# Row factors spread by two two-part products, first weights loaded in pieces by two queues, and an opening group's POOL products behind a quad's sums

## The chip, the cores and the metric

The kernel runs on one core of one Trainium2 chip. The metric is the device time of one execution in microseconds, the median of three runs. Times inside the kernel come from the trace of one profiled execution; there 0 is the start of its span. TensorE is called PE in the profile, VectorE DVE, ScalarE ACT, GpSimd POOL, and SP is the engine that issues most DMAs.

## The reference

One layer of a decoder trunk: 16 meta tokens and 2048 tokens of width 1024 are normalised and projected to eight groups of 512 columns; four of them feed a gated convolution, four a retention with rotary positions; the two results are joined, projected once more, added to the residual stream and normalised.

```python
hn = rms_norm(h, norm_g)
proj = jnp.einsum('bld,de->ble', hn, w_in)
cx, cb, cc, cg, q, k, v, rg = jnp.split(proj, N_PROJ, axis=-1)
conv_out = short_conv_branch(cx, cb, cc, conv_w) * jax.nn.silu(cg)
...
ret = head_group_norm(retention_chunkwise(qf, kf, vf), ret_norm_g)
ret_out = ret.astype(h.dtype) * jax.nn.silu(rg)
mixed = jnp.concatenate([conv_out, ret_out], axis=-1)
return h + jnp.einsum('ble,ed->bld', mixed, w_out)
```

`rms_norm` scales each token by the inverse root of its mean square (the *row factor* below) and each of the 1024 columns by a gain.

## The kernel before, in words

**Products.** All large products are made of fp32 numbers split into a high and a low part of type fp32r (`split`, `parts`): the high part is a rounded copy made by ScalarE, the low part the rest, made by VectorE. A product of 128x128 by 128x512 then takes three matmuls: low by high, high by low, high by high. Most products run as `quad`s: a 2x2 block product with seven instead of eight block products, whose sums of weights POOL makes (`stationary`; `summed[0]` is the last of a quad's four). The first two products of the first half of the tokens, and one at each later stage, run as `quad_plain`: eight block products without sums, in two passes over the tokens, each into two banks of PSUM: 2 passes x 2 banks x 8 tiles of 128 rows x 3 matmuls, 96 for one call. Four PSUM banks (`ps_proj`) serve these products, so the second `quad_plain` can begin only when the results of the first have been copied out of their banks (line 512 on ScalarE, line 507 on VectorE).

**The opening** (lines 909 to 945). `moving` loads the 16 blocks of x for the first half of the tokens and splits them, scaled by the column gain (line 113 ScalarE, line 114 VectorE; line 188 multiplies four blocks by the gain on ScalarE). `begin` loads the first group's weights and splits them (`plain_part`, lines 110 and 122). Ahead of them nine warming matmuls on a zeroed tile stand on TensorE (`warm_up`), behind ScalarE's first activation, which writes into the same tile (line 882). `normalise_meta` makes the meta tokens' factors (lines 405 to 420), `meta_products` multiplies weights by them (line 429). `block_sums` makes the sums of x blocks (line 185 on VectorE, and a subtraction of POOL's, line 122, tile `t`).

**Row factors** (`row_factors`, `spread_factors`, `spread`). The rows of x are loaded once more, two tiles of 128x512 for each 128 tokens (line 347), squared and summed on ScalarE (line 380), 16 times for 1024 tokens. From the sums of 512 tokens VectorE and POOL make one factor for each token (the power by POOL, line 305). To have the factors along the free dimension of every partition, `spread` multiplies the identity by the column of factors (line 312, VectorE), and one fp32 matmul with a column of ones (line 319) spreads the four diagonals of 128x128 over all partitions; ScalarE copies the result out and squares it (lines 322 and 324). It is called once for the meta tokens (16 columns) and four times for 512 tokens, twice in each half.

**The order of the work** is not written out: a scheduler orders each engine's queue by its own picture of the time, by the order of the program's text, and by `tc.issue_after`, which holds an instruction behind a named one. An engine works off its queue in that order.

**The opening group** (`group_plain`) is computed with the two plain products; what remains of it (`complete`, `close`) is done within the next unit: among it two products by the row factors on POOL (line 507, tile `c` by `rr`).

Of the kernel before, what the change touches and what calls it, by code (L numbers as in the profile page):

```python
# [28 lines left out]
RING, RAW, GEN, COPIES = 3, 8, 16, 4  # L29
WARM = 9  # L30
HIGH = 400
# [48 lines left out]
def hybrid_trunk(ctx: ExitStack, tc: tile.TileContext, t, out: bass.AP, chunk_decay):  # L80
# [23 lines left out]
    def brief(name="b"):  # L104
        return sb.tile([P, HB + 128], F32, name=name, tag="b", bufs=BRIEF)[:, :HB]

    def split(hi, lo, src, scale=None, eng=nc.vector):

        if scale is None:
            nc.scalar.copy(out=hi, in_=src)  # L110
            sub(eng, lo, src, hi.bitcast(F32))
            return
        nc.scalar.mul(hi, src, scale)
# [164 lines left out]
    def quad_plain(w, m, take, middle=None):  # L278

        for j in range(2):  # L280
            banks = [ps_proj() for _ in range(2)]
            for half in range(2):
                for kt in range(KH):
                    ks = slice(kt * P, (kt + 1) * P)
                    mh, ml = m[BLOCK[half][j]][kt]
                    for i in range(2):
                        wh, wl = w[2 * i + half]
                        for n, (a, b) in enumerate(((wl, mh), (wh, ml), (wh, mh))):
                            nc.tensor.matmul(  # L289
# [18 lines left out]
    def spread(col, n, dst, squares=None):  # L308

        a = col.shape[1]  # L310
        diag = sb.tile([P, HB], F32, name="rot", tag="rot", bufs=1).rearrange("p (a c) -> p a c", a=CH)
        nc.vector.tensor_tensor(
            out=diag[:n, :a, :n],
            in0=ident[:n, :n].rearrange("p (a c) -> p a c", a=1).broadcast_to([n, a, n]),
            in1=col.rearrange("p (a c) -> p a c", c=1).broadcast_to([n, a, n]),
            op=ALU.mult,
        )
        rp = ps_misc()
        nc.tensor.matmul(
            rp[:, : a * n].rearrange("p (a c) -> p a c", a=a), ones[:n].broadcast_to([n, P]), diag[:n, :a, :n], start=True, stop=True  # L320
        )
        nc.scalar.copy(out=dst, in_=rp[:, : a * n])
# [4 lines left out]
    ident = const.tile([P, P], F32, name="ident")  # L327
    ones = const.tile([P, 1], F32, name="ones")
    neg_half = const.tile([P, CH], F32, name="neg_half")
    meta_s = const.tile([P, KT, NMETA], F32, name="meta_s")  # L330
# [168 lines left out]
    def group_plain(g, m, f, meta, first, between, ahead):  # L499
# [30 lines left out]
        def complete():  # L530
# [4 lines left out]
            for j in range(2):  # L535
# [3 lines left out]
                nc.scalar.activation(gate, gate, AF.Silu)  # L539
                mul(nc.gpsimd, cs[j], cs[j], rr[j])  # L540

        def close():
            with tc.issue_after(turned[0].ins):
                for j in range(2):
# [270 lines left out]
    def output(pair, m, final_g):  # L815
# [41 lines left out]
        for i in range(2):  # L857
# [7 lines left out]
            for j in range(2):  # L865
# [9 lines left out]
                (nc.scalar if i == j and cuts[i] > 1 else nc.sync).dma_start(out[row : row + P, cs], y)  # L875

    make_identity(nc, ident)
    nc.gpsimd.memset(ones, 1.0)
    nc.gpsimd.memset(neg_half, -0.5)
    warm = const.tile([P, P], BF16, name="warm")  # L880
    nc.vector.memset(warm, 0.0)
    nc.scalar.activation(warm[:, 0:1], warm[:, 0:1], AF.Silu)

# [15 lines left out]

    warm_up(WARM)  # L900
    nc.sync.dma_start(gain, t["norm1_g"])
    factors = [[] for _ in range(NR)]
    held = {}
    for r in range(NR):
# [7 lines left out]
        if r == 0:  # L912
# [115 lines left out]
```

## Time and profile before

| what | value |
|---|---|
| median of 3 runs | 878.27 us (878.2 to 878.86) |
| the profiled execution | 878.86 us, its span 877.1 us |
| PE busy | 865.1 us, 99% of the span |
| DVE, ACT, POOL busy | 725.6, 472.3, 403.2 us |
| granted TensorE clock, mean | 0.998 |
| first matmul of a product | 6.29 us |
| first matmul of the first quad | 57.44 us |

A timeline row is start, length, engine, line, operation, output <- inputs, shapes and count; in brackets stands how long the engine was idle ahead of it and what ended that. A row of groups ends in the busy time, the mean length in ns, and the idle time ahead. A row of waits is the waiting engine with its tile and line, the one waited for, the sum, the count and the longest. A row of stretches has the stretch, its length, the busy time (and count) of PE, PEld, DVE, ACT and POOL, the granted clock, the DMA engines' share and GB/s. The opening and its row factors fill the first 57 of 877 us.

### The profile page before, as it was taken

To read this page: it belongs to the slowest core of one execution; us is meant where nothing else is said; L and a number is where in the kernel's file an instruction comes from. 1 tells how busy PE (TensorE), PEld (TensorE's weight loads), DVE (VectorE), ACT (ScalarE), POOL (GpSimd) and SP (SyncE) were. 2 spreads that over 40 slices of the span, in tenths; PEclk is the share of its full clock that TensorE was granted. 3 is DMA by queue.
4 is the path that set the end of the run, shared out by engine and by line. 5 is a ranking of instruction groups with operands and counts; after the bars stand their busy time and mean duration, and the time that the engine had idled before them with its cause. 6 is when DMAs were issued, how large, how long until landed. Compare 5 with 4: busy or idle time off the path is not lost.

```text
span 877.1 us, 12737 instructions
## 1 busy us (share of the span) xinstructions
PE 865.1 (99%) x4279; PEld 711.6 (81%) x4279; DVE 725.6 (83%) x1178; ACT 472.3 (54%) x873; POOL 403.2 (46%) x291
## 2 busy tenths in 40 slices
PE   8999999999999999999999999999999999999996
PEld 5777787878888778788888888888888888788885
DVE  6899888989887867999889898988767699757764
ACT  8665537364654645836464645544334475545453
POOL 0564242333235555552223323355646455877763
PEclk9999999999999999999999999999999999999999
DMA  9723224352556533935144353646222593555432
GB/s 331 230 72 83 64 71 136 113 151 96 124 189 180 184 117 111 307 109 146 52 112 149 97 166 84 207 108 206 72 72 61 164 352 115 175 165 184 155 121 84
DMA packets 110033, 125.31 MB, mean 143 GB/s; under 512 B 41424, under 2 KB 58128, under 8 KB 109968
## 3 DMA queue, kind: packets, MB, share of 16 engines
q1 hardware_dynamic: 109824, 124.24, 46.2%
q8 instruction: 34, 0.56, 0.3%
q14 instruction: 31, 0.25, 0.1%
q10 hardware_dynamic: 144, 0.26, 0.1%
HBM read 90.92 MB, written 25.17 MB: 132 GB/s over the span
## 4 chain that ended last, share of the span: by engine, by line
PE 87%; DVE 4%; DMA 3%; issue 2%; ACT 1%; SPq 1%; POOL 1%; POOLq 0%; DVEq 0%; ACTq 0%
PE pj L232 71%; PE pj L289 7%; PE ms L773 2%; PE ms L774 2%; PE ms L763 2%; PE ms L750 2%; DVE ml L122 1%; DMA x<-in_xT 1%; DMA w<-in_w_out 1%; PE ms L429 1%; PE ms L741 1%; SPq L393 1%; DVE ml L114 1%; DVE wl L122 1%; DMA ra<-mixed 1%
## 5 line engine op out<-in xcount | busy, mean ns | idle before, releaser
L232 PE MATMUL pj<-mh,wl 128*128 128x512 f32 x1008 | 398.6, 395 | 1.3 <-DVE wl L122 1.2
L232 PE MATMUL pj<-mh,wh 128*128 128x512 f32 x1008 | 393.2, 390 | 0.0
L232 PE MATMUL pj<-ml,wh 128*128 128x512 f32 x1008 | 392.7, 390 | 0.0
L110 ACT CAST wh<-ra 128x512 fp32r<-128x512 f32 x216 | 133.8, 620 | 266.8 <-PE pj L232 216.2
L232 PEld LDWEIGHTS pj<-mh,wl 128*128 128x128 f32 x1008 | 189.3, 188 | 44.0 <-issue 2.6
L122 DVE TENSOR_TENSOR wl<-ra,wh 128x512 fp32r<-128x512 f32 x216 | 192.2, 891 | 39.3 <-ACT wh L110 38.3
L232 PEld LDWEIGHTS pj<-mh,wh 128*128 128x128 f32 x1008 | 189.2, 188 | 39.9
L232 PEld LDWEIGHTS pj<-ml,wh 128*128 128x128 f32 x1008 | 189.4, 188 | 38.1 <-issue 0.5
L119 POOL TENSOR_TENSOR sa<-ra 128x512 f32<-128x512 f32 x36 | 54.9, 1525 | 102.1 <-DVE wl L122 42.2
L122 POOL TENSOR_TENSOR ra<-sa,ra 128x512 f32<-128x512 f32 x36 | 54.6, 1517 | 76.9 <-DVE wl L122 73.0
L122 POOL TENSOR_TENSOR ra<-ra 128x512 f32<-128x512 f32 x36 | 56.2, 1562 | 60.5 <-PE ms L429 51.6
L149 POOL TENSOR_TENSOR ra<-ra 128x512 f32<-128x512 f32 x36 | 57.3, 1593 | 32.4 <-issue 22.8
L239 ACT COPY tc<-pj 128x512 f32<-128x512 f32 x108 | 62.5, 579 | 0.0
L289 PE MATMUL pj<-ml,mh 128*128 128x512 f32 x128 | 50.3, 393 | 0.1
L289 PE MATMUL pj<-mh,mh 128*128 128x512 f32 x128 | 50.1, 392 | 0.0
L289 PE MATMUL pj<-mh,ml 128*128 128x512 f32 x128 | 49.0, 399 | 1.0 <-DVE ml L122 0.5
L786 POOL TENSOR_TENSOR rp<-rs,neg_half 128x4 f32<-128x4 f32 x16 | 17.8, 1111 | 56.0 <-DVE rs L119 55.9
L565 POOL TENSOR_TENSOR c<-c,rr 128x512 f32<-128x512 f32 x14 | 29.4, 2101 | 25.6 <-DVE c L606 14.4
L842 DVE TENSOR_TENSOR yo<-pj,yo 128x512 f32<-128x512 f32 (+1 forms) x33 | 22.0, 670 | 18.4 <-POOL yo L119 10.9
L844 ACT ACTIVATE rot<-yo 128x512 f32<-128x512 f32 (+1 forms) x33 | 20.3, 616 | 30.7 <-DVE yo L842 30.2
L565 POOL TENSOR_TENSOR c<-c,tc 128x512 f32<-128x512 f32 x14 | 27.8, 1988 | 18.0 <-ACT tc L591 14.9
L848 POOL TENSOR_TENSOR z<-yo,final_g 128x512 f32<-128x512 f32 x16 | 26.8, 1678 | 16.5 <-DVE yo L842 16.5
(140 smaller groups left out, 1215.4 us busy)
## 6 DMA issues: line engine op xcount, KB each, us to landing
ra<-in_w_in SPq DMA_DIRECT2D x128, 256.0 KB, 2.8
x<-in_xT SPq DMA_DIRECT2D x48, 256.0 KB, 4.7
w<-in_w_out SPq DMA_DIRECT2D x32, 256.0 KB, 5.1
ra<-mixed SPq DMA_DIRECT2D x32, 256.0 KB, 2.9
yo<-in_x SPq DMA_DIRECT2D x32, 256.0 KB, 4.5
ra<-in_x SPq DMA_DIRECT2D x16, 256.0 KB, 3.2
mixed<-c SPq DMA_DIRECT2D x16, 256.0 KB, 2.6
mixed<-qg SPq DMA_DIRECT2D x16, 256.0 KB, 2.3
```

The costliest lines, as they stand in the source:

```text
L110: nc.scalar.copy(out=hi, in_=src)
L119: eng.tensor_tensor(out=out, in0=a, in1=b, op=ALU.add)
L122: eng.tensor_tensor(out=out, in0=a, in1=b, op=ALU.subtract)
L149: summed[0] = nc.gpsimd.tensor_tensor(out=a12, in0=a12, in1=a11, op=ALU.subtract)
L232: nc.tensor.matmul(bank, a[:, ks], b, start=first and kt == 0 and n == 0, stop=kt == KH - 1 and n == 2, skip_group_check=not first,)
L239: copied[0] = nc.scalar.copy(out=c, in_=bank)
L289: nc.tensor.matmul(banks[i], a[:, ks], b, start=half + kt + n == 0, stop=half == 1 and kt == KH - 1 and n == 2,)
L565: eng.tensor_tensor(out=out, in0=a, in1=b, op=ALU.mult)
L786: nc.gpsimd.tensor_tensor(out=rp, in0=rs, in1=neg_half.rearrange("p (c a) -> p c a", a=1), op=ALU.pow)
L842: last[0] = nc.vector.tensor_tensor(out=y[:, cs], in0=pp[:, cs], in1=y[:, cs], op=ALU.add)
L844: nc.scalar.activation(junk[:, cs], y[:, cs], AF.Square, accum_out=at)
L848: nc.gpsimd.tensor_tensor(out=ys[i][j], in0=y, in1=final_g[:, j * HB : (j + 1) * HB], op=ALU.mult)
```

## The change

**Spread.** The factors are split in a high and a low part first (two instructions on 128x4, VectorE); the low part's diagonals are made by VectorE in one instruction as before, the high part's by ScalarE in one instruction for each 128 tokens, into a tile of their own; two fp32r matmuls with a column of ones in fp32r add them up. **Opening.** The column gains and the first 128 columns of two of the first weight tiles are loaded by ScalarE's queue, ahead of its activation table; the other 384 columns by SP, and the splits of these tiles are cut the same way. Warming takes ten matmuls and no longer waits for ScalarE. In `quad_plain` high by high comes first. `normalise_meta` is called after the twelfth x block instead of the eighth; the sums of x blocks are held behind the eighth scaled copy. **POOL.** The opening group's two products by the row factors move from `complete` to `close`, behind `summed[0]`.

```diff
-WARM = 9
+WARM = 10
...
-        nc.scalar.mul(hi, src, scale)
+        scaled.append(nc.scalar.mul(hi, src, scale))
...
-                        for n, (a, b) in enumerate(((wl, mh), (wh, ml), (wh, mh))):
+                        for n, (a, b) in enumerate(((wh, mh), (wl, mh), (wh, ml))):
...
     def spread(col, n, dst, squares=None):
 
         a = col.shape[1]
-        diag = sb.tile([P, HB], F32, name="rot", tag="rot", bufs=1).rearrange("p (a c) -> p a c", a=CH)
+        high, low = (small.tile([P, CH], t, name="ch", tag=f"ch{t}")[:n, :a] for t in (F32R, F32))
+        nc.vector.tensor_copy(out=high, in_=col)
+        sub(nc.vector, low, col, high.bitcast(F32))
+        diags = [sb.tile([P, HB], F32R, name="rot", tag="rot", bufs=1), gen("dg")[:, :HB].bitcast(F32R)]
+        lows, highs = (d.rearrange("p (a c) -> p a c", a=CH)[:n, :a, :n] for d in diags)
         nc.vector.tensor_tensor(
-            out=diag[:n, :a, :n],
+            out=lows,
...
-            in1=col.rearrange("p (a c) -> p a c", c=1).broadcast_to([n, a, n]),
+            in1=low.rearrange("p (a c) -> p a c", c=1).broadcast_to([n, a, n]),
             op=ALU.mult,
         )
+        for c in range(a):
+            nc.scalar.mul(highs[:, c], ident[:n, :n], high[:, c : c + 1].bitcast(F32))
         rp = ps_misc()
-        nc.tensor.matmul(
-            rp[:, : a * n].rearrange("p (a c) -> p a c", a=a), ones[:n].broadcast_to([n, P]), diag[:n, :a, :n], start=True, stop=True
-        )
+        for d, first in ((highs, True), (lows, False)):
+            nc.tensor.matmul(
+                rp[:, : a * n].rearrange("p (a c) -> p a c", a=a), ones_r[:n].broadcast_to([n, P]), d,
+                start=first, stop=not first,
+            )
...
-                mul(nc.gpsimd, cs[j], cs[j], rr[j])
 
         def close():
+            with tc.issue_after(summed[0].ins):
+                for j in range(2):
+                    mul(nc.gpsimd, cs[j], cs[j], rr[j])
...
+    nc.scalar.dma_start(gain, t["norm1_g"])
+
+    PIECES = slice(0, P), slice(P, HB)
+    opening = {n: raw() for n in (0, 2)}
+    for n, a in opening.items():
+        nc.scalar.dma_start(a[:, PIECES[0]], t["w_in"][2 * NG, n][:, PIECES[0]])
...
-    nc.scalar.activation(warm[:, 0:1], warm[:, 0:1], AF.Silu)
+    function = const.tile([P, 1], BF16, name="function")
+    nc.scalar.activation(function, warm[:, 0:1], AF.Silu)
...
-    nc.sync.dma_start(gain, t["norm1_g"])
...
             def begin(half):
-                for n in (half, 2 + half):
-                    w[n] = plain_part(n, loads[n], FIRST_W)
+                if half:
+                    for n in (1, 3):
+                        w[n] = plain_part(n, loads[n], FIRST_W)
+                    return
+                for n, a in opening.items():
+                    w[n] = a, operand(FIRST_W, n)
+                    nc.sync.dma_start(a[:, PIECES[1]], t["w_in"][2 * NG, n][:, PIECES[1]])
+                done = []
+                for cs in PIECES:
+                    with ExitStack() as behind:
+                        for ins in done:
+                            behind.enter_context(tc.issue_after(ins.ins))
+                        for n, a in opening.items():
+                            hi, lo = w[n][1]
+                            done = [
+                                nc.scalar.copy(out=hi[:, cs], in_=a[:, cs]),
+                                nc.vector.tensor_tensor(
+                                    out=lo[:, cs], in0=a[:, cs], in1=hi[:, cs].bitcast(F32), op=ALU.subtract
+                                ),
+                            ]
...
-                load_x(r), gain_of, {(0, 0): lambda: begin(0), (0, KH - 1): lambda: begin(1), (0, KT - 1): normalise_meta}
+                load_x(r), gain_of, {(0, 0): lambda: begin(0), (0, KH - 1): lambda: begin(1), (1, KH - 1): normalise_meta}
...
-                block_sums(b11, b12, b22, b21, t1[kt], t3[kt], gain_of(kt), gain_of(KH + kt), nc.gpsimd)
+                with tc.issue_after(scaled[KT - 1].ins):
+                    block_sums(b11, b12, b22, b21, t1[kt], t3[kt], gain_of(kt), gain_of(KH + kt), nc.gpsimd)
```

With its inputs changed, the scheduler orders the opening anew. On TensorE, at the second spread of 512 tokens in before (line 319, from the tile `rot`); line 289 are the plain products, tiles `mh` and `ml` the high and low parts, line 429 the meta products:

```order
L289 MATMUL pj<-mh_240,mh_292 128x512
L289 MATMUL pj<-mh_240,ml_299 128x512
L289 MATMUL pj<-ml_241,mh_298 128x512
L319 MATMUL ms<-rot,ones 128x512
L467 MATMUL ms<-ident,mk 128x16
L429 MATMUL ms<-ra,meta_s 16x128 x16
L289 MATMUL pj<-mh_240,mh_298 128x512
```

It stands within the second plain product; its first spread stands earlier in the same product. In the changed program, where line 291 are the plain products, 328 the spreads (of `dg`, the high diagonals, and `rot`, the low ones), 478 and 440 the transpose and the meta products:

```order
L291 MATMUL pj<-ml_270,mh_167 128x512
L328 MATMUL ms<-dg,ones_r 128x512
L328 MATMUL ms<-rot,ones_r 128x512
L328 MATMUL ms<-dg,ones_r 128x512
L478 MATMUL ms<-ident,mk 128x16
L440 MATMUL ms<-ra,meta_s 16x128 x16
L291 MATMUL pj<-mh_123,mh_297 128x512
L291 MATMUL pj<-mh_123,ml_298 128x512
L328 MATMUL ms<-rot,ones_r 128x512
L291 MATMUL pj<-ml_124,mh_297 128x512
```

The row `mh_123,mh_297` is the first of the second plain product: both spreads of the first half (the second one's low part excepted) and the second group's meta products now stand ahead of it, behind the last row of the first plain product.

On ScalarE, the last squares (line 380) and the first spread's copy (line 322) in before; line 110 are casts, line 512 the copy that frees a bank of the first plain product:

```order
L512 COPY u<-pj 128x512
L380 ACTIVATE ra,ss<-ra 128x512 x7
L435 COPY mk<-ms 16x128 x4
L380 ACTIVATE ra,ss<-ra 128x512 x4
L110 CAST mh_341<-x 128x512
L380 ACTIVATE ra,ss<-ra 128x512
L110 CAST mh_354<-x 128x512
L110 CAST wh<-ra 128x512
L110 CAST mh_345<-x 128x512
L110 CAST wh<-ra 128x512
L110 CAST mh_358<-x 128x512
L322 COPY rr<-ms 128x512
```

This copy of line 512, the second one, stands behind four of the 16 squares and ahead of the other twelve. In the changed program (squares are line 391, casts 112, the high diagonals 325, the bank copies of the first plain product 523):

```order
L391 ACTIVATE ra,ss<-ra 128x512 x3
L112 CAST mh_362<-x 128x512
L391 ACTIVATE ra,ss<-ra 128x512
L112 CAST mh_375<-x 128x512
L391 ACTIVATE ra,ss<-ra 128x512
L112 CAST wh<-ra 128x512 x2
L325 ACTIVATE dg<-ident,ch 128x128 x8
L523 COPY u<-pj 128x512 x2
L332 COPY rr<-ms 128x512
```

Both bank copies of the first plain product, and all eight diagonals, now stand behind the last square.

On SP, what follows the first x loads (line 404, with `in_w_in` the weights, line 358 the rows for the factors) in the changed program:

```order
L404 DMA x<-in_xT 128x512 x8
L418 DMA state_83<-in_metaT 128x128
L482 DMA ra<-in_w_in 128x512 x4
L930 DMA rot_t<-in_rot 128x2x1024
L965 DMA cols<-in_cols 128x12
L976 DMA causal<-in_causal 128x128
L977 DMA conv_w<-in_conv_w 128x12
L978 DMA ret_g<-in_ret_norm_g 128x4
L457 DMA mr<-in_rot_m 16x256
L404 DMA x<-in_xT 128x512 x4
L358 DMA ra<-in_x 128x512 x16
```

The last four x blocks stand behind the second group's weights, the rotary table and five small loads; in before all 16 x blocks were ahead of those.

More of the change, by code (lines that the diff above doesn't have):

```diff
@@ L105, in brief @@
         return sb.tile([P, HB + 128], F32, name=name, tag="b", bufs=BRIEF)[:, :HB]
+    scaled = []
     def split(hi, lo, src, scale=None, eng=nc.vector):
@@ L328, in hybrid_trunk @@
     ones = const.tile([P, 1], F32, name="ones")
+    ones_r = const.tile([P, 1], F32R, name="ones_r")
     neg_half = const.tile([P, CH], F32, name="neg_half")
@@ L879, in hybrid_trunk @@
     nc.gpsimd.memset(neg_half, -0.5)
+    nc.vector.tensor_copy(out=ones_r, in_=ones)
     warm = const.tile([P, P], BF16, name="warm")
     nc.vector.memset(warm, 0.0)
-    nc.scalar.activation(warm[:, 0:1], warm[:, 0:1], AF.Silu)
+    function = const.tile([P, 1], BF16, name="function")
+    nc.scalar.activation(function, warm[:, 0:1], AF.Silu)
     def warm_up(n):
```

## The prediction

> **What bounds the kernel now.** I read the page's first part, then who waited for whom on TensorE, then TensorE's timeline at the start and around the row-factor spreads.
>
> ```profile
> span 877.1 us, 12737 instructions
> PE 865.1 (99%) x4279; PEld 711.6 (81%) x4279; DVE 725.6 (83%) x1178; ACT 472.3 (54%) x873; POOL 403.2 (46%) x291
> ```
> ```profile
> PE ms L888 <- ACT warm L882: 2.3, 1, 2.3
> PE pj L232 <- DVE wl L122: 1.2, 2, 0.9
> PE pj L289 <- DVE ml L122: 0.5, 1, 0.5
> PE pj L289 <- ACT mh L113: 0.4, 1, 0.4
> ```
>
> TensorE is busy for 865.1 of 877.1 us, and its named waits add up to 4.4 us. So the time is a queue of matmuls. A gain can come only from an earlier first product, from fewer matmul passes, or from those few waits; a loss comes from anything that makes TensorE stand. What one product costs is read from the longest undisturbed stretch of the chain that ended last, and what the opening costs from TensorE's timeline (start, length, what, count, and in brackets the idle time before it).
>
> ```profile
> 577.69 114.27 PE pj L232 x504
> ```
> ```profile
> 2.29 4.02 PE L888 MATMUL ms<-warm 128*128 128x512 bf16 x9 [2.29 <-ACT warm L882]
> 6.29 0.79 PE L289 MATMUL pj<-mh,ml 128*128 128x512 f32 x1
> ...
> 7.15 0.40 PE L289 MATMUL pj<-mh,mh 128*128 128x512 f32 x1
> 7.39 0.39 PE L289 MATMUL pj<-mh,ml 128*128 128x512 f32 x1
> ```
> ```profile
> L888 PE MATMUL ms<-warm 128*128 128x512 bf16 x9 | 4.0, 631 | 2.3 <-ACT warm L882 2.3
> ```
>
> 504 products in 114.27 us are 0.2267 us each. In the opening nine matmuls of the same width take 4.02 us; each is 631 ns long, so they start (4.02 - 0.63) / 8, about 0.43 us, apart; from 7.15 on starts are 0.24 apart. An array that had stood idle ran at half rate for its first 4.0 us.
>
> **The parts that look like gains.** (a) The opening. The warming matmuls no longer wait for ScalarE's table (2.29) but for VectorE's zeroing of their operand.
>
> ```profile
> 0.82 0.11 DVE L881 MEMSET warm<- 128x64 uint32 x1 [0.82 <-PEq L1017]
> ```
> ```profile
> 0.74 0.40 SPq L901 DMA_DIRECT2D gain<-in_norm_g  x1
> 1.19 0.42 SPq L393 DMA_DIRECT2D x<-in_xT  x1
> ```
>
> Ten of them from 0.95 at 0.43 end at 5.3; the first x block moves up to the first issue (0.74 for 1.19), so ScalarE's first split comes at 3.7 instead of 4.12, and the first high parts are there before 5.3. First product 1.0 us earlier, and the waits of 0.5 and 0.4 on L289 may go too: 1.9 us at most. (b) Each spread of 512 row factors is one fp32 product before, two fp32r products after.
>
> ```profile
> 41.83 0.39 PE L289 MATMUL pj<-mh,mh 128*128 128x512 f32 x1
> 42.06 1.02 PE L319 MATMUL ms<-rot,ones 128*128 128x512 f32 x2
> 42.52 0.79 PE L289 MATMUL pj<-mh,ml 128*128 128x512 f32 x1
> 43.15 0.39 PE L289 MATMUL pj<-ml,mh 128*128 128x512 f32 x1
> ```
>
> From 41.83 to 43.15 stand two products and the spread, so it costs 1.32 - 0.45 = 0.87 us; two fp32r products cost 0.45. That is 0.42 each, 1.7 us for four. (c) POOL's products of the opening group sit between a quad's sums before, while VectorE's rotary halves last 1.67 us instead of 0.69 and its weight parts come late.
>
> ```profile
> 76.74 1.74 POOL L507 TENSOR_TENSOR c<-c,rr 128x512 f32<-128x512 f32 x1
> ```
> ```profile
> 77.36 1.67 DVE L622 TENSOR_TENSOR rot<-kv,rot_t 64x512 f32<-64x512 f32 x1
> ...
> 81.50 0.69 DVE L625 TENSOR_TENSOR kv<-kv,rot 128x512 f32<-128x512 f32 x1
> 82.11 0.69 DVE L122 TENSOR_TENSOR wl<-ra,wh 128x512 fp32r<-128x512 f32 x1
> ```
>
> This ends TensorE's longest wait on L232, 0.9 us, which goes. By these parts alone the change would win 1.0 + 0.9 + 1.7 + 0.9 = 4.5 us.
>
> **The part that decides.** The order of instructions in the changed program puts the first two spreads directly behind the 96 products of the first plain pass, and behind them the second pass's 96 products. In before they stood late within the second pass. The spread's operand comes from ScalarE, whose queue holds all 16 squares of the rows ahead of it, and the copies that free the banks of the second pass stand behind it too. So TensorE cannot start the second pass before ScalarE has worked off that queue. In before that did not matter, since TensorE came to the first spread at 42.06 only.
>
> How long is that queue? ScalarE's busy time from its first split to the end of the 16th square, in before (length, then busy time of PE, PEld, DVE, ACT, POOL), and the rows of what is added:
>
> ```profile
> 4.12:44.95 40.83, 40.31 (x205) 29.78 (x204) 33.20 (x57) 32.89 (x74) 13.85 (x6) 1.00 0.87 300
> ```
> ```profile
> 20.08 0.59 ACT L512 COPY u<-pj 128x512 f32<-128x512 f32 x1 [0.16 <-PE pj L289]
> 20.56 2.19 ACT L110 CAST mh<-ra 128x512 fp32r<-128x512 f32 x4
> ```
> ```profile
> L722 ACT ACTIVATE v<-v,rc 128x128 f32<-128x128 f32 x64 | 20.5, 391 | 0.4
> ```
>
> Of 40.83 us ScalarE works 32.9. The changed queue up to the last diagonal of the second spread holds the same work, less two bank copies (1.2), plus four casts more (two of sums, two of weights: 2.2), eight new 128x128 products by a column (nearest row L722: 20.5 / 64 = 0.32 each, 2.6), plus about 0.2 for cutting two casts in two: 36.7 us. Begun at 3.7 it ends at 40.4 if ScalarE never waits, and at 48.3 if it waits for the 7.9 us that it waited before. Which of its waits stay?
>
> ```profile
> ACT ra L380 <- DMA ra<-in_x: 3.0, 6, 0.9
> ACT mh L113 <- DMA x<-in_xT: 2.5, 3, 1.9
> ACT mh L110 <- PE pj L289: 2.3, 1, 2.3
> ```
>
> The 2.3 is a cast that waited for TensorE to finish with its buffer; it now stands among the squares, behind that. The 3.0 for rows I keep as a stand-in for what is new: the last four x blocks are now queued behind the rotary table and five small loads, and the second diagonal waits for POOL's power. That leaves 5.6 us of waits and the last diagonal at 46.0.
>
> TensorE comes there at about 30: 5.3 + 96 x 0.2267 = 27.1, and some 3 us: 0.9 of waits as before, 1.07 of meta products (row below), and about 1 for the norms' sums, the small spread and the later x blocks. It stands 16 us, less the two or three spread products that run as their operands come. Up to 30 every gain of part (a), and of the two early spreads in (b), is swallowed: TensorE only waits longer.
>
> What follows the last diagonal is read from before's rows:
>
> ```profile
> 35.95 1.07 PE L429 MATMUL ms<-ra,meta_s 128*16 128x128 f32 x32
> ...
> 53.20 0.23 PE L467 MATMUL ms<-ident,mk 16*128 16x16 f32 x1
> ...
> 57.44 0.39 PE L232 MATMUL pj<-mh,wl 128*128 128x512 f32 x1
> ```
>
> One spread product and its hand-over 0.3, the transpose 0.23, the meta products 1.07: 47.6. Then 97 products (96 and the last spread half) x 0.2267 = 22.0: 69.6. And the clock: what an idle array does is in the table of stretches (length, busy time and count of PE first, granted clock third from the end).
>
> ```profile
> 866.00:870.00 4.00, 3.81 (x17) 2.82 (x15) 1.16 (x4) 0.98 (x3) 1.08 (x2) 1.00 0.00 0
> 870.00:873.00 3.00, 0.00 (x0) 0.00 (x0) 2.13 (x7) 1.75 (x6) 0.55 (x1) 1.00 0.46 175
> 873.00:873.80 0.80, 0.00 (x0) 0.00 (x0) 0.26 (x1) 0.23 (x1) 0.00 (x0) 1.00 0.00 0
> 874.00:877.00 3.00, 0.00 (x0) 0.00 (x0) 0.00 (x0) 0.00 (x0) 0.00 (x0) 0.50 0.45 175
> ```
>
> The last matmul ends just before 870, and by 874 the granted clock is 0.50. So 14 us of standing halves the clock, and the opening shows what that costs: 4.0 us at 0.43 instead of 0.2267, 4.0 x (1 - 0.2267 / 0.43) = 1.9 us. About 1 us of those 4.0 passes with the first spread products ahead of the last wait, so I take 1.5 (bounds 0 and 1.9). The Trainium skill, "TensorE: Matmul & The Clock Gate", section "What's actually happening", has the default state throttled, entered again after an idle window of about 3.4 us and left after about 3.4 us of activity; by that figure the loss would be an estimated 1.6 us in full. The trace agrees with the rule, with about 4 us both ways.
>
> The first quad of the main loop (57.44 before) then starts at 69.6 + 1.5 = 71.1: 13.7 us later. Nothing of that is won back, as TensorE is full from there to the end. What remains as gain lies behind it: two spreads of the second half, 2 x 0.42 = 0.8, and the 0.9 of (c). Net 13.7 - 0.8 - 0.9 = 12.0 us.
>
> At nothing I cost: the tiny VectorE instructions of each spread (five times two, beside a TensorE that has products queued), the diagonals of the second half on ScalarE (it waits for TensorE there; 1.3 us each if that cover is gone), the loads by ScalarE's queue (three issues of about 0.42, SP's price, ahead of its table; if the table is not loaded when x lands, the queue of 36.7 us starts that much later), and the other order of the three terms. Of the scheduler's reshuffling at the second half's start I take nothing, with 0.8 either way.
>
> The profiled execution took 878.86 us, 1.8 beyond its span and 0.6 above the median of 878.27, which I forecast from: 878.27 + 12.0 = 890.3.
>
> **The rivals.** *No stall, faster.* If ScalarE delivered the diagonals by 30 us, when TensorE arrives, the gains of 4.5 us would stand: 873.8. Against it: 36.7 us of queued work from 3.7 on cannot be done by 30, waits or not. Only an order on the chip other than the program's would do it. 3 in 100. *A short stall.* ScalarE hardly waits, since half of its old waits were for rows whose loads may now run ahead: last diagonal at 40.4 to 43, so 3.0 to 5.6 us less than my forecast, 884.7 to 887.3; without the clock's loss too, 883.2. 17 in 100. *A longer stall, through POOL.* All four of POOL's subtractions of x blocks now stand ahead of the first power.
>
> ```profile
> 24.31 7.92 POOL L122 TENSOR_TENSOR t<-x 128x512 f32<-128x512 f32 x2 [5.05 <-DVE x L185]
> 35.90 1.03 POOL L305 TENSOR_TENSOR rc<-rs_v,neg_half 128x4 f32<-128x4 f32 x1 [3.67 <-DVE rs_v L302]
> ...
> 46.22 1.46 POOL L119 TENSOR_TENSOR sa<-ra 128x512 f32<-128x512 f32 x1 [0.31 <-ACT mh L110]
> ```
>
> Two took 7.92 us, beside VectorE. Ahead of the second pair VectorE has some 15 whole tiles at 0.69 from about 24 on, so it starts at about 34.4; if it lasts as long, powers and sum end at 34.4 + 7.9 + 1.0 + 1.5 + 1.0 = 45.8, the second factor's diagonals (1.3, and 0.5 of VectorE) at 47.6: 1.6 us more, 891.9; with all of ScalarE's old waits 892.6, with no later gain 894.3. The Trainium skill, "SBUF — State Buffer", section "Who interferes with whom", says that VectorE with two SBUF inputs and GpSimd lock each other out for whole instructions; 7.92 us for two such subtractions agrees. 15 in 100. *The change doesn't do what it says*, and the stall costs what the parts win: it would have to be 4 us long; 2 in 100.
>
> **How the numbers follow.** Main case, stall of some 15 us, 887.5 to 892.5: 63 in 100; short stall 17, long stall 15, faster 3, same 2. Range 884.5 to 894.3, from a short stall's bound to the long one's; the extreme without any wait and without the clock's loss (883.2) and the faster case are left out. A measurement of this kernel can tell about 0.2%, 1.8 us, from no change. Faster 0.03, same 0.02, slower 0.95.
>
> **What would show it.** TensorE's waits should hold a new row of some 12 to 17 us for a spread by ScalarE's diagonals, at about 30 us; L234's first product should start near 71; matmuls behind the stall should be 0.43 apart for up to 4 us. If that first quad starts before 57.4, I am wrong altogether. If the stall ends by 42, ScalarE's waits were mis-sized; if products run at 0.23 at once, the clock was. The two spreads of the second half should cost 0.45 each.

## The result, and the profile after

The changed kernel takes 899.21 us (median of 4 runs, 898.9 to 900.36), the kernel before 878.57 beside it (4 runs): ratio 1.0235, 95% interval 1.0217 to 1.0252, 20.6 us slower. Forecast were 890.3 and a range up to 894.3: the direction was right, the size was not.

First the page of the changed kernel and TensorE's waits in it:

```profile
span 897.1 us, 12766 instructions
PE 866.5 (97%) x4280; PEld 713.1 (79%) x4280; DVE 722.8 (81%) x1191; ACT 477.9 (53%) x892; POOL 393.7 (44%) x291
```
```profile
PE ms L328 <- ACT dg L325: 18.4, 2, 15.3
PE pj L234 <- ACT tc L241: 1.5, 1, 1.5
PE pj L234 <- DVE wl L124: 1.3, 2, 1.0
```

The span is 20.0 us longer and TensorE's busy time only 1.4: it stands. 18.4 us in two waits for the diagonals are new, and so is the wait for `tc`. Where the time was lost is read by comparing when the same product starts in both traces:

| start of | before | changed | difference |
|---|---|---|---|
| first product | 6.29 | 4.92 | -1.37 |
| second plain pass | 31.32 | 52.64 | +21.32 |
| first product of the first quad | 57.44 | 76.08 | +18.64 |
| quad product 673 | 243.79 | 262.26 | +18.47 |
| quad product 1009 | 334.01 | 351.81 | +17.80 |
| quad product 1177 (second half begun) | 396.01 | 413.09 | +17.08 |
| quad product 1345 | 442.06 | 462.18 | +20.12 |
| end of the last product | 869.81 | 890.00 | +20.19 |

So 18.6 us are lost before the first quad, 0.8 are won back up to product 1009, and 2.4 are lost at the start of the second half. TensorE's timeline around the stall:

```profile
4.92 0.50 PE L291 MATMUL pj<-mh,mh 128*128 128x512 f32 x1
...
29.65 0.61 PE L291 MATMUL pj<-ml,mh 128*128 128x512 f32 x2
45.55 0.80 PE L328 MATMUL ms<-dg,ones_r 128*128 128x512 f32 x1 [15.29 <-ACT dg L325]
...
49.86 0.80 PE L328 MATMUL ms<-dg,ones_r 128*128 128x512 f32 x1 [3.08 <-ACT dg L325]
...
50.80 1.91 PE L440 MATMUL ms<-ra,meta_s 128*16 128x128 f32 x32
52.64 0.80 PE L291 MATMUL pj<-mh,mh 128*128 128x512 f32 x1
...
54.94 0.63 PE L291 MATMUL pj<-mh,ml 128*128 128x512 f32 x1
55.37 0.45 PE L291 MATMUL pj<-ml,mh 128*128 128x512 f32 x1
```

TensorE is through the first pass at 30.26, as forecast, stands until 45.55 and, after one spread, again until 49.86. The 32 meta products take 1.91 us for 1.07. ScalarE and POOL in the same stretch:

```profile
41.72 1.12 ACT L112 CAST wh<-ra 128x512 fp32r<-128x512 f32 x2
44.22 1.28 ACT L325 ACTIVATE dg<-ident,ch 128x128 fp32r<-128x128 f32 x4 [1.38 <-DVE ch L314]
48.53 1.28 ACT L325 ACTIVATE dg<-ident,ch 128x128 fp32r<-128x128 f32 x4 [3.03 <-DVE ch L314]
49.83 1.07 ACT L523 COPY u<-pj 128x512 f32<-128x512 f32 x2
```
```profile
34.97 6.97 POOL L124 TENSOR_TENSOR t<-x 128x512 f32<-128x512 f32 x2 [4.95 <-ACT ra L391]
41.91 1.02 POOL L307 TENSOR_TENSOR rc<-rs_v,neg_half 128x4 f32<-128x4 f32 x1
42.89 1.27 POOL L121 TENSOR_TENSOR sa<-ra 128x512 f32<-128x512 f32 x1
46.74 1.55 POOL L307 TENSOR_TENSOR rc<-rs_v,neg_half 128x4 f32<-128x4 f32 x1 [2.58 <-DVE rs_v L304]
```

ScalarE has worked off its queue at 42.84, about when the forecast had it, and then waits 1.38 and 3.03 us for the split factors, which wait for POOL's two powers; the first of them stands behind two subtractions of x blocks. The copies that free the first pass's banks come last (49.83). The clock in short stretches (length, busy time of PE, PEld, DVE, ACT, POOL, granted clock, DMA):

```profile
34.00:35.00 1.00, 0.00 (x0) 0.00 (x0) 1.00 (x3) 0.83 (x4) 0.03 (x1) 0.99 0.93 328
35.00:36.00 1.00, 0.00 (x0) 0.00 (x0) 1.00 (x2) 0.67 (x3) 1.00 (x1) 0.50 1.02 389
...
54.00:55.00 1.00, 1.00 (x4) 0.72 (x3) 0.00 (x0) 0.67 (x2) 0.92 (x2) 0.50 0.00 0
...
55.50:57.00 1.50, 1.50 (x8) 1.23 (x7) 1.47 (x2) 0.62 (x1) 1.44 (x1) 1.00 0.04 11
```

It is halved at 35.0, 4.7 us after TensorE fell idle, and comes back at 55.5, 5.6 us after the last wait. The second loss, at the start of the second half, in rows of POOL, SP, ScalarE and TensorE of the changed kernel, and then POOL and SP in before:

```profile
406.94 5.23 POOL L151 TENSOR_TENSOR ra<-ra 128x512 f32<-128x512 f32 x1 [6.00 <-issue]
412.14 1.29 POOL L578 TENSOR_TENSOR c<-c,tc 128x512 f32<-128x512 f32 x1
```
```profile
405.63 8.20 SPq L490 DMA_DIRECT2D mixed<-c  x2
...
414.43 3.79 SPq L215 DMA_DIRECT2D t<-sums_x  x8
```
```profile
418.29 1.27 ACT L112 CAST mh<-t 128x512 fp32r<-128x512 f32 x2 [3.92 <-DMA t<-sums_x]
```
```profile
420.62 0.50 PE L234 MATMUL pj<-mh,wl 128*128 128x512 f32 x1 [1.48 <-ACT tc L241]
```
```profile
386.60 1.29 POOL L149 TENSOR_TENSOR ra<-ra 128x512 f32<-128x512 f32 x1 [3.21 <-issue]
```
```profile
387.10 2.90 SPq L479 DMA_DIRECT2D mixed<-c  x2
```

Read as a chain (e9 puts it to the test): one of POOL's sums takes 5.23 us for 1.29, the last product of the unit (`c` by `tc`) is late by that, SP's second store waits for it, the eight loads of sums stand behind the store, ScalarE waits for them, and the bank copy behind its casts lets TensorE stand.

### The profile page after: what moved, and what is told of

Its sections match the earlier page's. It is cut to its first block, busy times and chain, and to the rows that moved or that the text cites. A ratio compares the mean times of both kernels' runs of the same rounds, so it can differ in the third digit from the quotient of the medians.

```text
span 897.1 us, 12766 instructions
## 1 busy us (share of the span) xinstructions
PE 866.5 (97%) x4280; PEld 713.1 (79%) x4280; DVE 722.8 (81%) x1191; ACT 477.9 (53%) x892; POOL 393.7 (44%) x291
## 4 chain that ended last, share of the span: by engine, by line
PE 50%; DVE 1%; POOL 1%; issue 1%; DMA 1%; SPq 0%; POOLq 0%; DVEq 0%
PE pj L234 44%; PE pj L291 2%; PE ms L787 1%; PE ms L776 1%; PE ms L786 1%; PE ms L763 1%; DMA t<-sums_x 1%; DVE ml L124 1%; POOL yo L121 0%; PE ms L754 0%; DVE yo L855 0%; SPq L215 0%; POOL ra L124 0%; DVE yo L885 0%; POOL sa L121 0%
## 5 line engine op out<-in xcount | busy, mean ns | idle before, releaser
L124 DVE TENSOR_TENSOR wl<-ra,wh 128x512 fp32r<-128x512 f32 x216 | 186.6, 865 | 39.0 <-ACT wh L112 38.1
L124 POOL TENSOR_TENSOR ra<-ra 128x512 f32<-128x512 f32 x36 | 54.9, 1525 | 59.3 <-PE ms L440 51.4
L151 POOL TENSOR_TENSOR ra<-ra 128x512 f32<-128x512 f32 x36 | 61.4, 1706 | 36.2 <-issue 27.8
L291 PE MATMUL pj<-ml,mh 128*128 128x512 f32 x128 | 47.7, 393 | 0.0
L578 POOL TENSOR_TENSOR c<-c,rr 128x512 f32<-128x512 f32 x14 | 26.4, 1886 | 29.9 <-DVE c L619 18.1
L112 ACT CAST wh<-sa 128x512 fp32r<-128x512 f32 x36 | 22.1, 613 | 22.1 <-PE pj L234 22.1
```

The source lines that it names most:

```text
L124: eng.tensor_tensor(out=out, in0=a, in1=b, op=ALU.subtract)
L151: summed[0] = nc.gpsimd.tensor_tensor(out=a12, in0=a12, in1=a11, op=ALU.subtract)
L291: nc.tensor.matmul(banks[i], a[:, ks], b, start=half + kt + n == 0, stop=half == 1 and kt == KH - 1 and n == 2,)
L578: eng.tensor_tensor(out=out, in0=a, in1=b, op=ALU.mult)
```

## The experiments

Two theories on the first loss. *Queue*: ScalarE's eight diagonals and the later x loads put the second plain pass behind the spreads; this is how far the prediction had thought. *Ring*: the high diagonals lie in the ring of 16 buffers (`gen`), from which the two tiles `u` of the opening group are taken as well, and `u` then gets other buffers. In the program as built, the copies into `u` wait for other engines in the two kernels (before, then changed):

```
L512 COPY u<-pj 128x512 [waits DVE_49,PE_49]
L523 COPY u<-pj 128x512 [waits Pool_49] x2
```

**e1: before, with the old spread's diagonals in the ring.**

```diff
-        diag = sb.tile([P, HB], F32, name="rot", tag="rot", bufs=1).rearrange("p (a c) -> p a c", a=CH)
+        diag = gen("dg")[:, :HB].rearrange("p (a c) -> p a c", a=CH)
```

> The kernel before with one edit: the spread's diagonals lie in a buffer of the ring of 16 (tag g) instead of their own (rot); the spread itself stays one fp32 product of diagonals that VectorE makes. Theory Queue (the prediction's reason): the second plain pass came to stand behind the spreads because ScalarE got eight diagonals more and the last x blocks were loaded later; neither is here, so 877 to 880 us. Theory Ring (rival): the diagonals take the ring's buffers that the two tiles u had, u gets buffers that come free later, the scheduler therefore puts the copies into u, which free the banks of the first plain pass, behind the squares and the spreads ahead of the second pass. Then TensorE waits here too: in the changed kernel 15.3 + 3.1 us in the two waits and about 2.5 by the halved clock; without the eight diagonals and their waits for POOL's power somewhat less, 12 to 17 us: 890 to 896 us.

Measured: 901.24 us, ratio 1.0256 (1.0238 to 1.0273). This one line costs as much as the whole change. The rows are TensorE's:

```profile
48.12 2.04 PE L319 MATMUL ms<-dg,ones 128*128 128x512 f32 x2 [12.28 <-DVE rc L358]
51.82 0.79 PE L289 MATMUL pj<-mh,ml 128*128 128x512 f32 x1 [1.65 <-ACT u L512]
```

The new spread is not needed for the stall, the ring is enough. It is more than expected, since the squares now stand among the splits of x too, and the first pass ends at 35.8, in before at 31.5.

**e2: changed kernel, high diagonals in the ring of raw tiles.**

```diff
-        diags = [..., gen("dg")[:, :HB].bitcast(F32R)]
+        diags = [..., raw()[:, :HB].bitcast(F32R)]
```

> The changed kernel with one edit: the high diagonals lie in a buffer of the ring of raw tiles (tag ra, eight buffers) instead of the ring of 16. All eight diagonals by ScalarE, the later x loads and everything else stay. Queue: the same stall of 18 us, 896 to 900 us. Ring: the stall of 18.4 us and the halved clock go, the first quad starts near 57 instead of 76.1: 899.2 - 19 = 880, and 877 if the 3.0 us lost at 420 to 428 go with it: 876 to 881 us.

Measured: 884.36 us, 1.0058 (1.0043 to 1.0073). The second pass starts at 29.51 for 52.64, with all eight diagonals still ScalarE's: Queue is out. It is above Ring's range, because of a loss of 2.1 us between quad products 1009 and 1177 (waits of 1.07, 0.53 and 0.76) and of one wait that stays at the end of the pass:

```profile
56.57 0.50 PE L328 MATMUL ms<-ra,ones_r 128*128 128x512 f32 x1 [3.42 <-ACT ra L325]
```

**e3: before, with POOL's move alone.**

```diff
-                mul(nc.gpsimd, cs[j], cs[j], rr[j])
         def close():
+            with tc.issue_after(summed[0].ins):
+                for j in range(2):
+                    mul(nc.gpsimd, cs[j], cs[j], rr[j])
```

> The kernel before with the move of POOL's two products from complete to close alone. The prediction took 0.9 us for it: 877.4. The rival reading, from the changed kernel's wait of 1.0 at the same quad (101.4, where before had 0.9 at 82.9): the wait has another last cause and the move brings nothing, 877.9 to 878.7.

Measured: 879.46 us, 0.9999 (0.9989 to 1.0008). The profile shows why: the same wait is there, 0.72 us for 0.86, and only its last cause has changed.

```profile
81.81 0.47 PE L232 MATMUL pj<-mh,wl 128*128 128x512 f32 x1 [0.72 <-ACT wh L110]
```
```profile
82.94 0.47 PE L232 MATMUL pj<-mh,wl 128*128 128x512 f32 x1 [0.86 <-DVE wl L122]
```

**e4: changed kernel with the old spread,** the function `spread` as it was before:

```diff
-        for d, first in ((highs, True), (lows, False)):
...
+        nc.tensor.matmul(
+            rp[:, : a * n]..., ones[:n].broadcast_to([n, P]), diag[:n, :a, :n], start=True, stop=True
+        )
```

> The changed kernel with the old spread (one fp32 product, diagonals by VectorE in their own buffer); the new opening, the order of the terms, the later normalisation of the meta tokens and POOL's move stay. Queue: the eight diagonals are gone but the later x loads stay, so part of the stall stays, 882 to 892. Ring: no stall; the opening's first product 1.4 us earlier (4.92 for 6.29) is the whole difference to before, 876 to 878.5, and up to 880 if the 3.0 us at 420 to 428 come from the order of the terms.

Measured: 878.9 us, 0.9999 (0.9989 to 1.0008). No stall, no loss behind quad product 1177, and the first quad starts at 55.10 for 57.44, 2.3 us earlier. That is more than the opening brings: e7, e9 and e12 have the same instructions in the same order up to there and start it at 56.63, 56.35 and 56.46, and e3, with the old opening, at 56.45. In the mean the new opening wins 0.8 us, and single profiles lie 1 to 1.5 us apart. What is won is given back 7.5 us later:

```profile
62.63 0.69 PE L234 MATMUL pj<-mh,wl 128*128 128x512 f32 x1 [1.92 <-DVE wl L124]
63.12 0.63 PE L234 MATMUL pj<-ml,wh 128*128 128x512 f32 x1
...
66.10 0.41 PE L234 MATMUL pj<-mh,wh 128*128 128x512 f32 x1
```

VectorE is not through with the opening's splits when TensorE comes for the first quad's weights. It lets TensorE go on at 62.63 here and at 63.06, 62.70 and 62.83 in e7, e9 and e12: who comes earlier waits longer.

**e5: changed kernel, all x block subtractions by VectorE.**

```diff
-block_sums(b11, b12, b22, b21, t1[kt], t3[kt], gain_of(kt), gain_of(KH + kt), nc.gpsimd)
+block_sums(b11, b12, b22, b21, t1[kt], t3[kt], gain_of(kt), gain_of(KH + kt), nc.vector)
```

> The changed kernel with one edit: the subtractions of the sums of x blocks run on VectorE instead of POOL (the instruction order on TensorE and ScalarE stays as in the changed kernel). Theory POOL (the second diagonals came 3.8 us later than forecast since POOL's two last subtractions, 34.97 to 41.94, stand ahead of its first power): the first power starts near 39 to 40 instead of 41.9, the second diagonals end at 46 to 48 instead of 49.8, the first quad starts 2 to 3.5 us earlier than 76.1, and the time is 895.5 to 897.5. Rival, ScalarE's queue sets it (it ended at 42.8 in the changed kernel, and the second sum of squares is only read after its last square): first quad at 75 to 76.5, 898 to 900.

Measured: 895.96 us (2 runs), 1.0194 (1.0177 to 1.0212), first quad at 73.18. POOL's powers start at 39.25 and 44.26 for 41.91 and 46.74:

```profile
39.25 1.55 POOL L307 TENSOR_TENSOR rc<-rs_v,neg_half 128x4 f32<-128x4 f32 x1 [20.11 <-DVE rs_v L304]
...
44.26 1.33 POOL L307 TENSOR_TENSOR rc<-rs_v,neg_half 128x4 f32<-128x4 f32 x1 [0.24 <-DVE rs_v L304]
```

The theory POOL holds: the first quad starts 2.9 us earlier, 2.35 of them by the shorter wait (the second spread starts at 47.51 for 49.86) and the rest by a clock that comes back sooner. The edit turned VectorE's order as well: the second sum of squares now stands ahead of the first diagonals. So the 2.9 us belong to the subtractions and to that order together.

**e6: changed kernel with 42 matmuls in the wait.**

```diff
+        nc.vector.tensor_copy(out=warm[:, :CH], in_=behind)
+        for _ in range(fill):
+            nc.tensor.matmul(rp..., warm, warm..., start=True, stop=True)
```

> The changed kernel with 42 matmuls more on the zeroed warming tile, whose result is overwritten; they stand behind the first plain product and start when the first sum of squares is there (about 37.6). They should keep TensorE busy to about 49 in the wait. If the halved clock costs what the rows after the wait show (spread product, transpose and 32 meta products at half rate 1.2, five plain products at 0.43 for 0.23 1.0, and 0.5 more), the first quad starts 2 to 3 us earlier than 76.1: 896 to 897.5. If the clock costs only the 1.5 us of the prediction: 897.5 to 898. If it costs nothing, or the added matmuls delay the spread: 899 or more.

Measured: 898.27 us (2 runs, 897.04 and 899.51), 1.0221 (1.0202 to 1.0239). That lies between the second and the third case, and the time alone decides nothing. The trace tells more: the added matmuls began 4 us later than meant and ended 2.4 after the diagonals, but what follows runs at full clock.

```profile
41.81 10.72 PE L330 MATMUL ms<-warm 128*128 128x512 bf16 x42 [11.09 <-DVE warm L328]
...
52.84 0.39 PE L335 MATMUL ms<-dg,ones_r 128*128 128x512 f32 x1
```

From the second spread's first product to the first quad it takes 76.47 - 52.84 = 23.6 us here and 76.08 - 49.86 = 26.2 in the changed kernel, for the same work: the halved clock cost 2.6 us.

**e7: changed kernel, new spread for the second half's two alone;** `spread_one` is the old one.

```diff
-        spread(rc, P, rr, rr2)
+        (spread if r else spread_one)(rc, P, rr, rr2)
...
-        spread(rc[:NMETA, 0:1], NMETA, rr)
+        spread_one(rc[:NMETA, 0:1], NMETA, rr)
```

> The changed kernel with the old spread for the three of the opening and the new one for the two of the second half alone. Each new spread costs 0.42 us less on TensorE, as in the changed kernel (from +18.43 to +17.80 there): 0.6 to 0.8 us under the same kernel with the old spread throughout, which stood 1.0 us above before in its profile: 877.5 to 879. If the second half's loss of 2.3 us (420 to 428 in the changed kernel) comes from these two spreads' buffers in the ring of 16, it is here too: 880 to 882. If it comes from the opening's, it is absent.

Measured: 881.6 us, 1.0038 (1.0025 to 1.0051). Up to quad product 1009 it stands 0.1 us under before, then it loses 2.5: the loss at the second half is here, without any stall in the opening. (e4, without these two spreads, has none.)

**e8: e7, and four splits of sums in the first quad's first step.** `between` keeps the four of the fourth product, `later` makes those of the fifth.

```diff
-        return blocks, ((idle, idle, complete), idle, close)
+        return blocks, ((later, idle, complete), idle, close)
```

> The previous kernel, and four of the splits of sums (those of the fifth product of a quad) are held behind the first bank copy of the first quad instead of standing ahead of its weights on VectorE. With the old spread throughout, TensorE waited there 1.9 us for a low weight part and then ran 8 products at 0.43: 2.4 + 1.5 = 3.9 us, all of the 2.3 us that the opening had gained by then and more. If VectorE's queue is the cause, this wait shrinks below 1 us and the clock stays up: 3 to 3.9 us less than the previous kernel, 874 to 875.5, faster than before by 0.35 to 0.5%. If the held splits themselves become late for the fifth product, 877 to 880.

Measured: 880.9 us, 1.0023 (1.0013 to 1.0033): 0.7 less than e7 with intervals that overlap, and not 3. The wait only moves on to a later weight part, 1.3 us at 67.6.

**e9: e7, with the last unit's two results stored by POOL's queue.**

```diff
-            store_mixed(r, j, g, cs[j])
+            store_mixed(r, j, g, cs[j], nc.sync if r or g != UNITS[0][-1] - NG else nc.gpsimd)
```

> The kernel with the new spread in the second half alone (e7), with one edit: the last convolution unit of the first half stores its two results by POOL's queue instead of SP's; the instructions of TensorE, VectorE and ScalarE keep their order. Theory Chain: at the start of the second half POOL's last product of that unit came late (394.16, behind a sum of weights that took 5.23 us beside VectorE), SP's store waited for it (8.2 us for two), the eight loads of sums stood behind the store on SP (396.5), ScalarE waited for them and the bank copy behind its casts was late: 1.75 us of TensorE, and 1.25 us behind that. With the store off SP's queue the loads go out about 3 us earlier, the first of the two waits goes and perhaps the second: 1.7 to 3.0 us less than e7's 881.6: 878.6 to 879.9. Rival: TensorE's two waits come from VectorE's and ScalarE's order alone: no change, 881 to 882.

Measured: 880.41 us, 1.0019 (1.0011 to 1.0028), for e7's 1.0038. In the profile the stretch from quad product 1177 to 1345 takes 46.92 us, in e7 49.09, in before 46.05; the wait of TensorE for `tc` is gone. POOL's sum is as slow as before, but the loads no longer stand behind it:

```profile
388.58 5.22 POOL L151 TENSOR_TENSOR ra<-ra 128x512 f32<-128x512 f32 x1
393.76 1.29 POOL L596 TENSOR_TENSOR c<-c,tc 128x512 f32<-128x512 f32 x1
```
```profile
394.20 4.21 SPq L215 DMA_DIRECT2D t<-sums_x  x8
```

The chain holds for the first of the two waits; a second, of a low weight part, keeps 0.9 us. The median came out 0.5 us above the expected range; it is 1.2 us under e7's, and the two intervals just touch, so the 2.2 us rest on the profile.

**e10: e4 with e8's edit** (`later` for the first `idle`).

> The changed kernel with the old spread everywhere (e4), and four splits of sums held behind the first bank copy of the first quad, as in e8. e4 had the opening's gain of 2.3 us at the first quad and lost 3.7 behind it, 2.4 in a wait for a low weight part and about 1.5 at the halved clock. e8 still had a wait of 1.6 there, at full clock. So about 2.4 us less than e4: 1.3 us under before, 876.5 to 878, which is within or just beyond what can be told from before. If the wait stays long enough to halve the clock: 878.5 to 879.5.

Measured: 878.73 us, 1.0001 (0.9992 to 1.001). The first quad starts 2.0 us earlier than in before, and at quad product 169 nothing of it is left: one wait of 1.80, at full clock. The time is above the 876.5 to 878 expected for a full clock.

```profile
66.13 0.39 PE L234 MATMUL pj<-mh,wh 128*128 128x512 f32 x1
68.31 0.47 PE L234 MATMUL pj<-mh,wl 128*128 128x512 f32 x1 [1.80 <-ACT c L495]
```

**e11: changed kernel, a buffer of its own for the high diagonals.**

```diff
-RING, RAW, GEN, COPIES = 3, 8, 16, 4
+RING, RAW, GEN, COPIES = 3, 8, 15, 4
...
-gen("dg")[:, :HB].bitcast(F32R)
+sb.tile([P, HB], F32R, name="dg", tag="dg", bufs=1)
```

> The changed kernel with a buffer of its own for the high diagonals and 15 instead of 16 buffers in the ring, which the space of SBUF just allows. All instructions of the change stay. Theory Ring: the ring is one buffer shorter instead of being entered by the diagonals; the first bank copy then stands ahead of ScalarE's squares again and the second behind ten of them (in the changed kernel both behind all 16 and the eight diagonals); the second plain pass starts at 33 to 38 instead of 52.6, and a wait stays for the second spread: 880 to 886. Theory Queue: 896 to 900, as ScalarE has the same diagonals to make.

Measured: 885.72 us, 1.0078 (1.0064 to 1.0092), second pass at 29.46, first quad at 52.95, 4.5 us before the old one (1.7 of it since the second spread and its meta products now come behind the quad's first products). Then TensorE stands for a low weight part and runs 5.4 us at half rate:

```profile
65.71 0.80 PE L234 MATMUL pj<-mh,wl 128*128 128x512 f32 x1 [5.31 <-DVE wl L124]
...
71.00 0.46 PE L234 MATMUL pj<-mh,wl 128*128 128x512 f32 x1
```

Ring again, and e4's lesson in a larger size: however early TensorE is at the first quad, VectorE lets it go on at some 63 to 66 us.

**e12: e4, the second half's two diagonals in the ring.** `spread`, for the second half alone, is the one of e1:

```diff
+        diag = gen("dg")[:, :HB].rearrange("p (a c) -> p a c", a=CH)
...
+        (spread if r else spread_one)(rc, P, rr, rr2)
```

> The changed kernel with the old spread (one fp32 product) everywhere; the diagonals of the second half's two lie in a buffer of the ring of 16. It tells what of the new spread brings the second half's loss (from the 1177th to the 1345th quad product e4 took 46.03 us and e7 49.09 us): Ring: the buffers, so about 3 us are lost there as in e7, 881 to 882. Instructions: the four diagonals by ScalarE, the two products and their earlier readiness, which change the order of the loads and of VectorE; the diagonals' place alone changes nothing there: 46.0 us, and 878 to 880 in all.

Measured: 880.24 us, 1.0014 (1.0004 to 1.0024). From quad product 1177 to 1345 it takes 46.06 us: no loss there, so the diagonals' place alone does not bring it. The new spread's instructions alone don't either: e2 and e11 keep both new spreads of the second half, with the diagonals outside the ring, and take 46.06 and 46.03 us. Those that lose 2.4 to 3.0 us there, the changed kernel and e5 to e8, have both. How the two together turn the order of the loads is not settled. The place has a price of its own a little earlier: from product 1009 to 1177 e12 takes 62.81 us and e4 61.53, for a wait that e4 doesn't have.

```profile
370.24 0.50 PE L291 MATMUL pj<-mh,ml 128*128 128x512 f32 x1 [1.35 <-DVE ml L124]
```

No version beats the kernel before by more than a measurement can tell.

## Why the prediction was wrong

The order had been read rightly: TensorE came to the spreads at 30.3 (forecast about 30), stood there for ScalarE's diagonals, and the gains up to there were swallowed. The sum was 8.2 us short at the end of the products (12.0 forecast, 20.2 measured), in four terms.

- **"That leaves 5.6 us of waits and the last diagonal at 46.0."** It ended at 49.81, 3.8 later. ScalarE's queue had been sized well (done at 42.84); what ended last was the chain behind it, POOL's subtractions, power, sum and second power. The rival *A longer stall, through POOL* had the mechanism and 15 in 100; it had the subtractions ending at 42.3 (41.94) and missed that POOL then waits 2.58 us for VectorE, which has two splits queued ahead of the second sum of squares. e5, without the subtractions and with that sum ahead, starts the first quad 2.9 us earlier.
- **"so I take 1.5 (bounds 0 and 1.9)" for the clock.** It cost 2.6 (e6). The bound of 1.9 came from an opening in which TensorE works without pause; here the second wait of 3.08 us fell into the recovery, and the spread products ahead of it, which the forecast had counted as part of the recovery, did not shorten it. The clock came back 5.6 us after that wait, not 4.0. The 4.0 were read too short as well: in before's opening the clock is halved from 2.29, where TensorE starts, to 6.94, 4.65 us, with the first product (6.29) still in it.
- **"and the 0.9 of (c)".** The wait stays at 0.72 (e3): ScalarE's weight cast is the next to be late there, only 0.14 us sooner than what had ended the wait. What was late next had not been asked.
- **"Of the scheduler's reshuffling at the second half's start I take nothing, with 0.8 either way."** It cost 2.4 us: 3.0 from product 1177 to 1345, less 0.7 won just ahead. e7 loses the 3.0 with the second half's new spreads alone; e4 without them, e12 with their place alone, and e2 and e11 with the spreads outside the ring don't. e9 wins back 2.2 of them through SP's queue.

Added up: 13.7 + 3.8 + 1.1 = 18.6 at the first quad; less 0.2 and 0.7, plus 2.4, gives 20.1 at the end of the products (20.2 measured). Right was the spread's price (0.42 forecast): in before the second one of the second half takes 1.09 with one product, so 0.86, and in the changed kernel 0.47, as these rows of the two show. Of the opening's 1.0 + 0.9, the first is right (the first product is 1.4 earlier), while at the first quad 0.8 is left in the mean of the profiles.

```profile
356.20 1.02 PE L319 MATMUL ms<-rot,ones 128*128 128x512 f32 x2
356.65 0.79 PE L232 MATMUL pj<-mh,wl 128*128 128x512 f32 x1
357.29 0.39 PE L232 MATMUL pj<-ml,wh 128*128 128x512 f32 x1
```
```profile
379.44 0.40 PE L328 MATMUL ms<-dg,ones_r 128*128 128x512 f32 x1
379.67 0.40 PE L328 MATMUL ms<-rot,ones_r 128*128 128x512 f32 x1
379.91 0.39 PE L234 MATMUL pj<-mh,wl 128*128 128x512 f32 x1
```

What the prediction had not seen at all is the cause of the order: it took the changed order as given. e1, e2 and e11 show that the stall hangs on where one scratch tile lies. That the scheduler turns the order since the buffers of `u` come free later in its picture is argued from the waits as built; that the place of the tile does it is shown. The waits don't settle it, for in the traces of e1 and e5 the same copies are as late (51.18 and 47.48) and carry no wait for another engine.

## What to carry to other kernels

A scratch tile that is taken from a shared ring is an edit to every later user of the ring: look at who gets which buffer and at the order of instructions before counting what the edit saves. A gain at the start of a kernel is worth what the next engine to be late leaves of it; here VectorE had no room at 60 to 68 us, so neither the 1 to 2 us of the new opening nor the 4.5 of e11 arrived at the end. Keep stores that wait for a late result off the queue on which the next stage's loads stand.

## What the hardware showed

The clock fell sooner than expected in one place: in e4 TensorE stood 1.9 us (60.70 to 62.63) and ran its next eight products 0.43 apart; in e10 1.8 us of standing left the clock full, and in the changed kernel the clock was full for 4.7 us of standing. It came back after 3.5 us of work (e4), 5.4 (e11) and 5.6 (changed). The Trainium skill, "TensorE: Matmul & The Clock Gate", section "What's actually happening", gives windows of about 3.4 us that run free of the kernel. The traces agree with the windows: the granted clock changes on one grid, for its stretches at half speed inside the kernels last 3.41 us (e2, e4), 6.83 (e11), 10.24 (e6), 13.65 (e1), 17.07 (e5) and 20.48 (changed), all multiples of 3.413. That it takes an idle window to let the clock fall, as the prediction has it from there, they don't bear out: it fell behind windows in which TensorE was busy for 44% (e4) and 31% (e2) of the time, and held behind 45% (e1), 49% (e2) and 55% (e10). It came back behind windows that were busy for 79% (e2, in the opening), 87% (e1), 89% (e6) and more, and not behind 60% (e1) and 64% (changed). So here it is the busy share of a window that counts, and a wait of 1.9 us costs by where it falls on the grid. The shares are read from matmuls whose ends are modelled, so the 44 and 45% only say that the limit lies near there.

POOL was slowed beside a VectorE in full work: the third subtraction took 5.75 us and the fourth 1.25 (together the 6.97 above), where the first two took 1.88 and 1.67; a sum took 5.23 that took 1.29 in before, and it ended 1.15 us after VectorE's unbroken run of work did (411.02). Where POOL came first, VectorE was the one to wait: beside the first two subtractions its instructions of 0.74 took 1.79 and 1.78. In e5, with the subtractions moved to VectorE, each takes 0.68 us. The Trainium skill, "SBUF — State Buffer", section "Who interferes with whom", has a VectorE instruction with two SBUF inputs contend with a GpSimd instruction that reads SBUF, for a shared port pair that is an exclusive lock; the traces agree in kind.
